# Attention probabilities divided by their sum on GpSimd in place of VectorE

## The chip, the cores and the metric

One core of one Trainium2 chip. The metric is the device time of one execution in microseconds (us). The engines are named as the profile names them: PE is TensorE, DVE is VectorE, ACT is ScalarE, POOL is GpSimd, SP is the engine that issues most DMAs.

## The reference, cut to what matters

A two-layer encoder of 1024 positions and width 1024 in float32. The first layer mixes by windowed attention with 16 query heads on 4 key heads, the second by a gated recurrence; each is followed by layer norm, a gated feed-forward block and a gated side input. The change lies in the attention of the first layer. For each block of 128 queries, with the keys of the block itself and its two neighbours:

```python
s = jnp.einsum('bqhgd,bkhd->bhgqk', qb, kb) * scale
s = jnp.where(valid, s, -jnp.inf)
m = jnp.maximum(s.max(-1, keepdims=True), sink_f)
pr = jnp.exp(s - m)
den = pr.sum(-1, keepdims=True) + jnp.exp(sink_f - m)
return jnp.einsum('bhgqk,bkhd->bqhgd', (pr / den).astype(vb.dtype), vb)
```

Inputs of the attention are x, the weights of the projections and one sink value per head.

## The kernel before, in words

**Matmuls.** Each float32 operand is split into a high part, a cast by ACT (L73), and a low part, the difference, by DVE or POOL (L74, the helper `split`). A product is three matmuls, high by high, high by low and low by high (L349 to L351, the helper `mm3`).

**A group of attention** is one block b of 128 queries and one j, half of the heads (eight heads, as four t by two r). There are sixteen groups. In `scores`, for each t, PE makes two tiles of scores (L562, up to 128x384, in PSUM), and DVE takes scale, mask and row maximum in one pass and puts the scores in SBUF (L564, tiles `pr`; in the first three groups `pq`). When all eight tiles are there, DVE works out the maximum with the sink (L568) and its negative (L570), ACT makes eight exponentials with their row sums (L578), DVE adds the sink's term (L579) and takes the reciprocal (L580, `den`, 128x8), and then eight instructions scale the eight tiles in place, each by one column of `den` (L584). They go through the tiles with t outside and r inside. Blocks 0 and 7 have two key blocks and tiles of 128x256, the other six have three and 128x384: four narrow groups and twelve wide.

**The values** (`values`) of a group come one group later. For each r and each key block, PE transposes four tiles, one for each t, into one PSUM tile (L607, `tps`). ACT and DVE split it into `ph` and `pl` (L73, L74), and PE multiplies both with the value block (L595, L596, tile `o`). ACT and DVE put the result into `of` (L599, L600); its split into `oh` and `ol` ends in POOL (L615 by way of L74; the trace calls these tiles `qh` and `ql`).

**What runs beside it.** `groups` interleaves the scores of one group with the values of the group before, step by step. `weave` puts in 1.15 steps of `more` for each of those: the remaining projections of queries, keys and values, and later the output projection (`aops`, L626). A projected tile of queries or keys is rotated in `rotate`: a shuffle by DVE (L484), a product by POOL (L485), a product and a sum by DVE (L487, L488), and a split that ends in POOL. Of a weight tile `w_qkv` the first half is split by DVE and the second by POOL; of `w_ao` likewise in the first half of the output projection.

**What sets the order.** Each engine runs its queue in order. The order in the queue is not the order of the source alone: when the program is built, the framework places the instructions of each engine by their dependencies and by its own idea of their times. So instructions of `more` stand between those of a group on every engine.

Of the kernel before, what the change touches and what calls it, by code (L numbers as in the profile page):

```python
# [33 lines left out]
def build(tc, xT, pT, wqkv, watt_o, whg, wvh, whg_o, wfi, wfo, wpg, wpp, sink, lbl, ngd, lnp,  # L34
          rope, amask, hmask, ident, outT):
    nc = tc.nc
    sync, act, dve, pool, pe = nc.sync, nc.scalar, nc.vector, nc.gpsimd, nc.tensor
# [8 lines left out]
    with (  # L46
# [16 lines left out]
        def A(name, dt=F32):  # L63
            return ap_.tile([P, HALF], dt, tag="a", name=name)
# [401 lines left out]
        def attention(X, Y):  # L466
            with (
# [70 lines left out]
                def scores(b, j):  # L538
                    h, c = divmod(b, 4)
                    kbs = [kb for kb in (b - 1, b, b + 1) if 0 <= kb < NB]  # L540
                    n = len(kbs)
                    m0 = kbs[0] - (b - 1)
                    if b in (3, 4):
                        kt, ko = Km[j], (b - 3) * P
                    else:
                        kt, ko = Kt[j][h], (kbs[0] % 4) * P
                    kh, kl = (z[:, ko:ko + n * P] for z in kt)
                    mx = tp.tile([P, 2, 4], F32, tag="mx", bufs=3, name="mx")
                    early = j == 0 and b < 3
                    if early:  # L550
                        pq = [qp.tile([P, 4, HALF], F32, tag="q", bufs=8, name=f"pq{r}") for r in range(2)]
                        ss = [pq[r][:, t] for t in range(4) for r in range(2)]
                    else:
                        ss = [A("pr") for _ in range(8)]
                    for t in range(4):
                        yield
                        sp = [aps.tile([P, 3 * P], F32, tag="s", bufs=2, name=f"s{i}") for i in range(2)]
                        qh, ql = (z[:, t, c * P:(c + 1) * P] for z in Q[j][h])
                        for i, (qq, kk) in enumerate(((qh, kh), (qh, kl), (ql, kh))):
                            for r in range(2):  # L560
                                rs = slice(64 * r, 64 * r + 64)
                                pe.matmul(sp[r][:, :n * P], lhsT=qq[rs], rhs=kk[rs], start=i == 0, stop=i == 2)  # L562
                        for r in range(2):
                            dve.tensor_tensor_reduce(ss[2 * t + r][:, :n * P], sp[r][:, :n * P],  # L564
                                                     am[:, m0 * P:(m0 + n) * P], HD ** -0.5, -1e30,
                                                     ALU.add, ALU.max, mx[:, r, t:t + 1])
                    sk = snk[:, 2 * j:2 * j + 2]
                    dve.tensor_tensor(mx, mx, sk, op=ALU.max)  # L568
                    ng = tp.tile([P, 2, 4], F32, tag="ng", bufs=2, name="ng")
                    dve.tensor_scalar_mul(ng, mx, -1.0)  # L570
                    es = tp.tile([P, 2, 4], F32, tag="es", bufs=2, name="es")
                    dve.tensor_tensor(es, sk, mx, op=ALU.subtract)
                    act.activation(es, es, AF.Exp)
                    den = tp.tile([P, 2, 4], F32, tag="den", bufs=2, name="den")
                    for t in range(4):
                        for r in range(2):
                            pt = ss[2 * t + r][:, :n * P]
                            act.activation(pt, pt, AF.Exp, bias=ng[:, r, t:t + 1], accum_out=den[:, r, t:t + 1])  # L578
                    dve.tensor_tensor(den, den, es, op=ALU.add)  # L579
                    dve.reciprocal(den, den)  # L580
                    for t in range(4):
                        for r in range(2):
                            pt = ss[2 * t + r][:, :n * P]
                            dve.tensor_scalar_mul(pt, pt, den[:, r, t:t + 1])  # L584
                    return b, j, kbs, ss

                def values(b, j, kbs, ss):
# [53 lines left out]
                def groups(gs):  # L641
                    prev = None
                    for g in gs:
                        box = []

                        def first(g=g, box=box):
                            box.append((yield from scores(*g)))

                        if prev is None:
                            yield from first()  # L650
                        else:
                            yield from both(first(), values(*prev))
                            seen.add(prev[:2])
                        prev = box[0]
                    yield from values(*prev)
# [682 lines left out]
```

## Time and profile before

| | |
|---|---|
| median of three runs | 2872.57 us (2869.69 to 2874.74) |
| profiled execution | 2872.11 us |
| its span, first to last instruction | 2870.3 us |
| mean granted clock of PE | 0.981 of full speed |

The time of a run is a little longer than the span, which leaves out what lies before the first and behind the last instruction. All times inside the profile count from the span's start. An engine's busy time holds only instructions that compute; what it waited for is inferred from the semaphores.

### The profile page before, as it was taken

To read this page: it belongs to the slowest core of one execution; us is meant where nothing else is said; L and a number is where in the kernel's file an instruction comes from. 1 tells how busy PE (TensorE), PEld (TensorE's weight loads), DVE (VectorE), ACT (ScalarE), POOL (GpSimd) and SP (SyncE) were. 2 spreads that over 40 slices of the span, in tenths; PEclk is the share of its full clock that TensorE was granted. 3 is DMA by queue.
4 is the path that set the end of the run, shared out by engine and by line. 5 is a ranking of instruction groups with operands and counts; after the bars stand their busy time and mean duration, and the time that the engine had idled before them with its cause. 6 is when DMAs were issued, how large, how long until landed. Compare 5 with 4: busy or idle time off the path is not lost.

```text
span 2870.3 us, 37158 instructions
## 1 busy us (share of the span) xinstructions
PE 2711.7 (94%) x12820; PEld 2184.5 (76%) x12820; DVE 2007.5 (70%) x2903; ACT 1287.1 (45%) x2338; POOL 1407.1 (49%) x982
## 2 busy tenths in 40 slices
PE   8999998999999998999998999989989999999998
PEld 6666676788887787787787877878767888878777
DVE  6778887755554657848888888898885554556685
ACT  4555666333333445534444443444553333344453
POOL 4243234756555747653433433331466565566563
PEclk9999999999999999999999999999999999999999
DMA  4111135544445943211111211112355444478243
GB/s 162 50 44 45 51 113 186 168 162 165 148 157 194 358 159 110 85 59 64 56 63 45 74 55 59 60 52 78 111 172 180 158 156 141 157 272 300 82 156 115
DMA packets 194301, 360.35 MB, mean 126 GB/s; under 512 B 22080, under 2 KB 24896, under 8 KB 194112
## 3 DMA queue, kind: packets, MB, share of 16 engines
q1 hardware_dynamic: 150048, 277.74, 29.0%
q10 hardware_dynamic: 44064, 80.24, 7.7%
q8 instruction: 101, 1.65, 0.2%
q14 instruction: 88, 0.72, 0.1%
HBM read 273.47 MB, written 84.41 MB: 125 GB/s over the span
## 4 chain that ended last, share of the span: by engine, by line
PE 33%; DVE 11%; issue 5%; POOL 4%; DMA 3%; ACT 2%; SPq 0%; ACTq 0%; POOLq 0%; DVEq 0%
PE x L349 3%; PE x L351 3%; PE x L350 3%; PE zps L351 2%; PE zps L350 2%; PE zps L349 2%; PE lv L1078 2%; POOL wo L74 2%; PE op L1158 1%; DVE K L1075 1%; PE zy L349 1%; PE zy L351 1%; PE zy L350 1%; DMA wraw<-w 1%; DVE Q L1048 1%
## 5 line engine op out<-in xcount | busy, mean ns | idle before, releaser
L74 POOL TENSOR_TENSOR w_hz<-r_hz,w_hz 128x512 fp32r<-128x512 f32 x128 | 180.3, 1415 | 333.0 <-ACT w_hz L73 322.5
L74 DVE TENSOR_TENSOR wp<-wraw,wp 128x512 fp32r<-128x512 f32 x204 | 216.0, 1059 | 167.0 <-ACT wp L73 137.9
L74 DVE TENSOR_TENSOR hs<-wraw,hs 128x512 fp32r<-128x512 f32 x154 | 206.3, 1356 | 144.7 <-ACT hs L73 141.5
L74 POOL TENSOR_TENSOR wo<-wraw,wo 128x512 fp32r<-128x512 f32 x154 | 226.2, 1481 | 157.4 <-ACT wo L73 153.5
L73 ACT CAST wp<-wraw 128x512 fp32r<-128x512 f32 x204 | 126.6, 622 | 282.3 <-PE x L351 142.4
L349 PE MATMUL x<-xc,wp 128*128 128x512 f32 x528 | 211.2, 401 | 8.0 <-DVE u L757 8.0
L351 PE MATMUL x<-xc,wp 128*128 128x512 f32 x528 | 211.2, 400 | 3.9 <-DVE wp L74 3.9
L349 PE MATMUL zps<-xh_n,w_hz 128*128 128x512 f32 x512 | 212.7, 415 | 0.0
L350 PE MATMUL x<-xc,wp 128*128 128x512 f32 x528 | 210.4, 399 | 0.5 <-DVE xc L74 0.5
L351 PE MATMUL zps<-xh_n,w_hz 128*128 128x512 f32 x512 | 202.7, 396 | 0.0
L350 PE MATMUL zps<-xl_n,w_hz 128*128 128x512 f32 x512 | 201.7, 394 | 0.0
L73 ACT CAST wo<-wraw 128x512 fp32r<-128x512 f32 x154 | 95.4, 620 | 187.8 <-POOL wo L74 114.2
L186 POOL TENSOR_TENSOR wraw<-s,wraw 128x512 f32<-128x512 f32 x36 | 47.6, 1322 | 217.4 <-DVE wp L74 204.8
L349 PE MATMUL ox<-hs,wo 128*128 128x512 f32 x352 | 138.7, 397 | 12.2 <-ACT hs L73 12.2
L351 PE MATMUL ox<-hs,wo 128*128 128x512 f32 x352 | 139.0, 395 | 1.6 <-POOL wo L74 1.6
L350 PE MATMUL ox<-hs,wo 128*128 128x512 f32 x352 | 139.1, 395 | 0.4 <-DVE hs L74 0.4
L349 PEld LDWEIGHTS x<-xc,wp 128*128 128x128 f32 x528 | 100.4, 190 | 34.7 <-ACT wp L73 5.8
L1078 PEld LDWEIGHTS lv<-Q,ks 128*128 128x128 f32 x768 | 97.9, 191 | 37.4 <-issue 23.1
L1070 ACT COPY ks<-K 128x512 f32<-128x512 f32 x96 | 60.5, 631 | 144.7 <-DVE K L1075 111.7
L1078 PE MATMUL lv<-Q,ks 128*128 128x128 f32 x768 | 105.5, 280 | 20.6 <-DVE tot L1089 10.2
L351 PEld LDWEIGHTS x<-xc,wp 128*128 128x128 f32 x528 | 100.4, 190 | 29.4 <-DVE wp L74 4.8
L73 ACT CAST w_hz<-r_hz 128x512 fp32r<-128x512 f32 x128 | 79.0, 618 | 89.6 <-issue 42.4
(377 smaller groups left out, 8475.4 us busy)
## 6 DMA issues: line engine op xcount, KB each, us to landing
wraw<-in_wfi_dram SPq DMA_DIRECT2D x192, 256.0 KB, 3.6
wraw<-in_wfo_dram SPq DMA_DIRECT2D x154, 256.0 KB, 4.0
wraw<-h SPq DMA_DIRECT2D x154, 256.0 KB, 4.8
r_hz<-in_whg_dram SPq DMA_DIRECT2D x128, 256.0 KB, 2.8
wraw<-w SPq DMA_DIRECT2D x88, 256.0 KB, 5.3
w<-wraw ACTq DMA_DIRECT2D x66, 256.0 KB, 2.1
h<-th ACTq DMA_DIRECT2D x66, 256.0 KB, 2.1
r_pg<-in_wpg_dram SPq DMA_DIRECT2D x32, 512.0 KB, 4.2
```

What stands on the lines that cost most here:

```text
L73: act.copy(hi, src)
L74: (eng or dve).tensor_tensor(lo, src, f32(hi), op=ALU.subtract)
L186: pool.tensor_tensor(a11, tmp, a11, op=ALU.subtract)
L349: pe.matmul(ps, lhsT=w[0], rhs=x[0], start=start, stop=False, skip_group_check=free)
L350: pe.matmul(ps, lhsT=w[0], rhs=x[1], start=False, stop=False, skip_group_check=free)
L351: pe.matmul(ps, lhsT=w[1], rhs=x[0], start=False, stop=stop, skip_group_check=free)
L1048: dve.tensor_tensor(Qq[:, 1 - d], qk[:, 0], Fg[:, d], op=ALU.mult)
L1070: act.copy(view(ks, 0, [[2 * B, g], [B, 2], [1, B]]), kv)
L1075: dve.tensor_tensor(kv, kv, view(cur, off + 1, [[2, g], [row - 1, 2], [0, B]]), op=ALU.mult)
L1078: pe.matmul(lv[:, c], lhsT=ks[:, c * P:(c + 1) * P], rhs=view(Qq, c * P, dims), start=True, stop=True)
L1158: pe.matmul(op[:, cs], lhsT=a, rhs=b, start=i == 0, stop=i == len(ops) - 1)
```

## The change

Line 584 is issued to POOL in place of DVE. The operands, the loop around it and everything else in the source stay as they are.

```diff
                     for t in range(4):
                         for r in range(2):
                             pt = ss[2 * t + r][:, :n * P]
-                            dve.tensor_scalar_mul(pt, pt, den[:, r, t:t + 1])
+                            pool.tensor_scalar_mul(pt, pt, den[:, r, t:t + 1])
                     return b, j, kbs, ss
```

## Rows read from the trace of the kernel before

**Rows 1.** The page: the span, and busy us, share and instructions of PE.

```profile
span 2870.3 us, 37158 instructions
PE 2711.7 (94%) x12820; PEld 2184.5 (76%) x12820; DVE 2007.5 (70%) x2903; ACT 1287.1 (45%) x2338; POOL 1407.1 (49%) x982
```

**Rows 2.** One window: length, busy us of five engines, PE clock, DMA share, GB/s.

```profile
60.00:390.00 330.00, 309.09 (x1545) 222.84 (x1546) 263.00 (x685) 189.77 (x478) 102.74 (x81) 0.97 0.16 53
```

**Rows 3.** The instructions of L584: duration ns min/median/max, first and last start.

```profile
L584 DVE TENSOR_SCALAR pr<-pr,den x104: 342/409/1532, 137.1 to 376.2; 128x384 f32<-128x384 f32 x80, 128x256 f32<-128x256 f32 x24
L584 DVE TENSOR_SCALAR pq<-pq,den x24: 340/405/1433, 76.4 to 121.3; 128x384 f32<-128x384 f32 x16, 128x256 f32<-128x256 f32 x8
```

**Rows 4.** PE's waits, 60 to 400 us: us in total, times, longest.

```profile
PE tps L607 <- DVE pr L584: 6.5, 7, 2.0
PE s L562 <- DVE mx L564: 6.4, 3, 4.4
PE o L596 <- DVE pl L74: 5.0, 4, 2.5
PE tps L607 <- DVE pq L584: 3.4, 4, 1.9
PE aops L350 <- POOL ql L74: 0.8, 1, 0.8
```

**Rows 5.** Timeline of DVE: start, duration, instructions.

```profile
76.35 4.22 DVE L584 TENSOR_SCALAR pq<-pq,den 128x256 f32<-128x256 f32 x8
...
88.25 0.72 DVE L484 STREAM_SHUFFLE sw<-qps 128x512 f32<-128x512 f32 x1
...
178.61 4.76 DVE L584 TENSOR_SCALAR pr<-pr,den 128x384 f32<-128x384 f32 x8
...
231.08 5.91 DVE L584 TENSOR_SCALAR pr<-pr,den 128x384 f32<-128x384 f32 x8
...
301.52 2.71 DVE L584 TENSOR_SCALAR pr<-pr,den 128x384 f32<-128x384 f32 x8
...
374.32 2.19 DVE L584 TENSOR_SCALAR pr<-pr,den 128x256 f32<-128x256 f32 x8
```

**Rows 6.** Timeline of POOL: start, duration, instruction, idle time before it and its end.

```profile
89.12 1.29 POOL L485 TENSOR_TENSOR sw<-sw,rt 128x512 f32<-128x512 f32 x1 [10.01 <-DVE sw L484]
...
162.60 0.40 POOL L510 CAST kmh<-kh 128x256 fp32r<-128x256 f32 x1
...
231.19 1.46 POOL L74 TENSOR_TENSOR ql<-ra,qh 128x512 fp32r<-128x512 f32 x1 [3.19 <-ACT qh L73]
232.81 1.29 POOL L74 TENSOR_TENSOR w_qkv<-r_qkv,w_qkv 128x512 fp32r<-128x512 f32 x1 [0.16 <-ACT w_qkv L73]
```

**Rows 7.** Timeline of PE, transposes and value products.

```profile
80.36 0.65 PE L607 MATMUL tps<-idn,pq 128*128 128x128 f32 x2
...
181.78 0.33 PE L607 MATMUL tps<-idn,pr 128*128 128x128 f32 x1 [1.83 <-DVE pr L584]
...
183.52 0.41 PE L607 MATMUL tps<-idn,pr 128*128 128x128 f32 x1
...
237.64 0.80 PE L596 MATMUL o<-pl,v 128*128 128x512 f32 x1 [2.54 <-DVE pl L74]
...
262.64 0.49 PE L596 MATMUL o<-pl,v 128*128 128x512 f32 x1 [1.69 <-DVE pl L74]
...
304.57 0.38 PE L607 MATMUL tps<-idn,pr 128*128 128x128 f32 x2
```

**Rows 8.** Windows behind four of those waits, columns as in rows 2.

```profile
81.00:84.50 3.50, 3.50 (x12) 1.98 (x10) 2.29 (x8) 0.96 (x2) 0.00 (x0) 0.59 0.05 16
182.00:186.50 4.50, 4.50 (x18) 3.43 (x17) 3.20 (x9) 1.50 (x3) 2.05 (x2) 0.62 0.19 62
239.00:242.00 3.00, 3.00 (x14) 2.69 (x13) 2.41 (x6) 2.29 (x5) 1.89 (x2) 0.69 0.00 0
262.70:266.00 3.30, 3.30 (x18) 2.63 (x19) 3.09 (x6) 1.79 (x3) 1.43 (x2) 1.00 0.19 67
```

## The prediction

> **What bounds the kernel now.** The page comes first [rows 1]: TensorE (PE) is busy 94% of the span. So the kernel is bound by PE as a whole, and an edit on DVE or POOL is worth only what PE loses by waiting for them. Next come the windows of the attention stretch, the only one in which the edited line runs [rows 2]: from 60 to 390 us PE is busy 309.09 of 330 us and its granted clock is 0.97 on average; DVE is busy 263.00 us (80%), POOL 102.74 us (31%). PE's idle time there is 20.9 us. A clock of 0.97 means that 3% of the time was lost at the lower of the two levels, 1.2 against 2.4 GHz: some 10 us. So no edit in this stretch that leaves PE's work alone can win more than about 31 us, 1.1% of the time. That is a ceiling, not a forecast.
>
> Then the list of PE's own waits there [rows 4]: 9.9 us go to transposes (tps, L607) that wait for the scaling of L584 (6.5 for the tiles pr, 3.4 for pq), 6.4 us to scores waiting for the reduction L564, 5.0 us to the value product waiting for DVE's split pl. The timelines show why the scalings are late [rows 5, 6, 7]. In the group at 301.52, during which POOL starts nothing, eight scalings of 128x384 take 2.71 us: one every 0.34 us. In the group at 231.08 POOL runs its subtractions beginning at 231.19 and 232.81, and the same eight take 5.91 us. The reader should see both halves of this: the eight are a block in DVE's in-order queue, so whatever stands behind them (pl above all) is late too. The wait of 2.54 us at 237.64 and that of 1.69 us at 262.64 are such pl's behind a block.
>
> What a wait costs beyond itself is in the clock [rows 8]. In the stretches that follow the waits of 1.8 us and more (81 to 84.5 us, 182 to 186.5, 239 to 242) PE's granted clock is 0.59 to 0.69; a fourth like the second begins at 207 and has 0.60. In the stretch behind the wait of 1.69 us at 262.64 it is 1.00. The time lost is the stretch by (1 - clock): 3.5 x 0.41 = 1.4 us, 4.5 x 0.38 = 1.7, 3.0 x 0.31 = 0.9, and for the fourth 4.0 x 0.40 = 1.6.
>
> **The change part by part.** *Removed from DVE:* 128 instructions in 16 groups of eight [rows 3]; the blocks last from about 2.2 to 5.91 us [rows 5], some 60 us of DVE's 263. This alone gives PE nothing except where PE waited for something queued behind a block. Those are the pl waits, 2.54 + 1.69 us and 0.2 us in a third place, 4.4 us of the 5.0 in the list, and the slow clock behind the first: 0.9 us from 239 to 242 and about 0.3 us just before. Together that is 5.6 us, and I take all of it as won, since the list names DVE's pl as what came last there.
>
> *Added to POOL:* the same 128 instructions, at a price that no row shows, since POOL runs no such operation before. From below: one of its casts of 128x256, which also read one tensor and write one, takes 0.40 us where DVE doesn't disturb it [rows 6]; were that all fixed cost, 384 columns would take 0.40 too, and were it all columns, 0.60. From above: its subtractions of 128x512 take 1.29 us, so 384/512 of that is 0.97 us, for an operation with two inputs. I take 0.55 us for 384 columns and 0.40 for 256, in the cast's span and near its upper end, because the scaling reads one tensor as the cast does. For the first instruction I add 0.15 us, the gap between the end of a shuffle on DVE (88.25 + 0.72) and the POOL instruction at 89.12 that it releases [rows 5, 6]. The k-th scaling of a wide group thus ends 0.15 + 0.55k us after the point at which DVE starts today; the seventh, which the last transposes of the first key block need, at 4.0 us; in a narrow group (256 columns) at 2.95 us.
>
> The Trainium skill (GPSIMD Engine Reference, section 4.1 Engine selection) speaks against such a move: elementwise work belongs on VectorE, GpSimd being about twice as slow with two inputs, though roughly at line rate with one. Twice DVE's undisturbed 0.34 would be an estimated 0.68 us, and by the slope worked out below the sum would shrink from 10 to about 2 us. No row here shows which half of the rule holds for a scaling with one scalar per partition; the casts lean to its second half.
>
> *The transposes.* Nine groups have waiting or tight transposes at the head of their values. For each I take when the transposes with t = 3 start today, counted from the start of the block, against 4.0 us (2.95 if narrow) [rows 5, 7]. At 178.61 they start at 183.52, 4.9 us in: 0.9 us won. In the next one, at 203.75 and of the same pattern, they come 5.8 us in: 1.8 won. At 76.35 (narrow; 80.36, 4.0 in): 1.05 won. At 301.52 (304.57, 3.05 in): 0.95 lost. At 374.32, the last group and narrow, 2.0 in: 0.9 lost, with little left to cover it. The other four (100, 118, 158 and 283 us, from 3.5 to 4.1 in) come to 0.95 lost together. Net: 0.95 us won. The gaps are also smaller, since four transposes share them: below the 1.69 us behind which the clock stayed up. So of the three slow stretches at 81, 182 and 207 I count as won what is not already in these figures: 1.4 + 1.1 + 0.8 = 3.3 us.
>
> The SBUF — State Buffer page of the Trainium skill (section Who interferes with whom) says that a DVE instruction using both ports blocks GpSimd entirely and is blocked by it. The trace agrees with 5.91 against 2.71 us for the same block. By it the stretching would vanish with the move; the sum above needs only the blocks as measured.
>
> *What is queued behind it on POOL.* POOL is in order. Its subtractions ql and w_qkv become ready at the same moment as the scalings (231.19 beside 231.08), as the two starts show. Behind eight scalings they come 4.4 us later. Their readers are scores of a later group, the output projection, or the next weight tile. PE waits 0.8 us for POOL in the whole stretch, once [rows 4], and I cost this at nothing, hidden by the projections' matmuls; uncovered it would be up to 4 us a group.
>
> **The sum**, against the profiled execution's own 2872.11 us (span 2870.3), half a microsecond from the runs' median of 2872.57: 5.6 + 0.95 + 3.3 = 9.85 us won, so 2862.3, rounded to 2862. Each 0.1 us on the price of one scaling moves the seventh by 0.7 us in nine groups, 6 us in all; the gain is used up at about 0.71 us.
>
> **The rivals.**
>
> *A: nothing measurable.* The order within each engine's queue is laid out anew when the program is built, for all engines. PE may then wait elsewhere (as it does for 6.4 us on L564) as long as it did. For it: PE is busy 94% anyway. Against it: eleven waits on the scalings and three on a pl behind them, 14 us in all, hang on these blocks alone. Time: 2867 to 2877.
>
> *B, slower: POOL's scaling is dear.* At 0.97 us the seventh ends 6.95 us in, 2.95 us later than in my sum, in nine groups: 26 us, and nine waits beyond 1.8 us with 1.5 us of slow clock each: 13. Time: 2862 + 39 = 2901. It decides from 0.71 us on; at 0.80 it gives 2862 + 15 = 2877 without any slow clock and 2890 with all of it. For it: POOL's subtractions of 1.29 us. Against it: its casts.
>
> *C: POOL's one queue.* If one or two subtractions of 1.29 us stand ahead of the scalings in the nine groups in which both become ready together, transposes come 12 to 23 us later in total: 2874 to 2885. For it: the coincidence in time. Against it: today the block starts 0.11 us before the first of them [rows 5, 6], so the scalings are ready first.
>
> **How the numbers follow.** Forecast 0.40 (own range 2855 to 2869), A 0.25, B 0.22, C 0.13. A change under 0.2% (5.7 us) can't be told from none here. Faster takes 0.36 of the forecast and 0.04 of A: 0.40. Same takes 0.04 of the forecast, 0.20 of A and 0.05 of C: 0.29. Slower is all of B, 0.08 of C and 0.01 of A: 0.31. The range goes from 2855, the forecast's low end, to 2903, just past B at 0.97 us.
>
> **What would show it.** On POOL, L584 at 0.5 to 0.6 us for 384 columns, eight in a row without a subtraction between them; at 0.75 or more the forecast fails. Among PE's waits, pl near zero, tps on POOL's L584 at 5 to 10 us in shorter pieces, and a mean clock from 60 to 390 us of 0.98 or more. DVE's busy time there should fall by some 60 us. Were tps waits at 25 us or more, B or C would hold, told apart by the mean duration and by what stands between the scalings. Were all this as described and the time unchanged, PE's idle time in the stretch would name the new wait.

## The result and the profile after

| | before | after |
|---|---|---|
| median | 2873.18 us (2869.69 to 2874.74, 4 runs) | 2992.30 us (2989.11 to 2993.78, 4 runs) |
| span of the profiled execution | 2870.3 us | 2991.3 us |
| mean granted clock of PE | 0.981 | 0.957 |

The kernel became slower: 1.042 times the time before, 95% interval 1.0407 to 1.0433, some 119 us. The prediction said 2862, range 2855 to 2903.

The first lines of the page of after, beside [rows 1]:

```profile
span 2991.3 us, 37207 instructions
...
PE 2771.3 (93%) x12820; PEld 2214.6 (74%) x12820; DVE 1961.0 (66%) x2775; ACT 1288.2 (43%) x2338; POOL 1549.3 (52%) x1110
```

POOL has 142 us more of work, DVE 46.5 us less, although the 128 scalings took 59.2 us there: other instructions of DVE take longer now, the sum L488 above all (22.9 us in twenty, 15.9 before). The last scaling starts at 495.8 us (376.2 before), so all of the loss lies in the attention. The instructions of L584, beside [rows 3]:

```profile
L584 POOL TENSOR_SCALAR pr<-pr,den x104: 917/1242/1849, 160.8 to 495.8; 128x384 f32<-128x384 f32 x80, 128x256 f32<-128x256 f32 x24
L584 POOL TENSOR_SCALAR pq<-pq,den x24: 922/1237/1706, 78.7 to 139.7; 128x384 f32<-128x384 f32 x16, 128x256 f32<-128x256 f32 x8
```

The median is 1.24 us, that of the wide tiles, and the shortest, 0.92, that of the narrow ones. DVE's undisturbed 0.34 [rows 5] is 3.7 times shorter. The attention as one window, beside [rows 2], 450 us where it was 330:

```profile
60.00:510.00 450.00, 363.94 (x1528) 251.07 (x1529) 214.77 (x555) 189.42 (x475) 246.40 (x209) 0.80 0.12 38
```

PE is idle for 450 - 363.94 = 86 us (21 before), and its granted clock is 0.80 (0.97): of 364 busy us a fifth, 73 us, is lost to the lower level (9 before). That is 65 us more idle and 64 us more of slow clock; together 129, a little above the 120 by which the stretch grew. PE's waits, 60 to 520 us, beside [rows 4]:

```profile
PE tps L607 <- POOL pr L584: 59.0, 42, 2.1
PE tps L607 <- POOL pq L584: 14.1, 12, 2.0
PE s L562 <- DVE mx L564: 6.7, 3, 4.8
PE o L596 <- DVE pl L74: 6.5, 3, 4.0
```

Fifty-four waits of transposes on a scaling, 73.1 us, stand where eleven with 9.9 us stood; every one of the sixteen groups has two to four. The 63 us more are nearly all of PE's added idle time. The waits for pl have not gone. The same list over all engines:

```profile
ACT ph L73 <- PE tps L607: 149.4, 42, 8.6
DVE pl L74 <- ACT ph L73: 74.7, 31, 7.2
```

Before, these two rows had 50.6 and 5.1 us. One group of after shows how the waits come about, in the timeline (start, duration, instruction, idle time before it and what ended it):

```profile
105.72 0.20 DVE L580 RECIPROCAL den<-den 128x8 f32<-128x8 f32 x1
...
106.09 10.18 POOL L584 TENSOR_SCALAR pq<-pq,den 128x384 f32<-128x384 f32 x8 [6.39 <-ACT qh L73]
...
107.39 0.44 PE L607 MATMUL tps<-idn,pq 128*128 128x128 f32 x2 [1.06 <-POOL pq L584]
...
109.33 0.20 DVE L568 TENSOR_TENSOR mx<-mx,snk 128x8 f32<-128x8 f32 x1
...
110.22 0.44 PE L607 MATMUL tps<-idn,pq 128*128 128x128 f32 x2 [1.84 <-POOL pq L584]
...
112.66 0.69 PE L607 MATMUL tps<-idn,pq 128*128 128x128 f32 x2 [1.22 <-POOL pq L584]
...
115.11 0.69 PE L607 MATMUL tps<-idn,pq 128*128 128x128 f32 x2 [1.33 <-POOL pq L584]
...
115.62 1.07 ACT L73 CAST ph<-tps 128x512 fp32r<-128x512 f32 x2 [8.58 <-PE tps L607]
...
116.24 1.29 DVE L74 TENSOR_TENSOR pl<-tps,ph 128x512 fp32r<-128x512 f32 x2 [6.71 <-ACT ph L73]
...
122.35 0.17 DVE L570 TENSOR_SCALAR ng<-mx 128x8 f32<-128x8 f32 x1
...
124.17 0.61 ACT L578 ACTIVATE pq<-pq,ng 128x384 f32<-128x384 f32 x1
```

Read it from the top. POOL's eight take 10.18 us with nothing between them. PE's queue holds the transposes in pairs, one pair for each t (one transpose for each of two key blocks), with at most a few matmuls between two pairs, so PE stops four times. ACT's cast ph stands at the head of ACT's queue for 8.58 us until the last pair is done, and DVE's pl waits behind it. Here the maximum of the *next* group is ready at 109.33 + 0.20, but its negative (L570) stands behind pl and part of a rotation in DVE's queue and comes at 122.35, and its exponentials follow at 124.17.

So the block of one group holds up the reciprocal, and with it the block, of the next. In most groups, however, this goes another way. There are fifteen passages from a group to the next, and in fourteen of them the negative starts 0.2 to 3.5 us after the maximum; it is the maximum itself that is late, because the scores are. The group whose reciprocal starts at 189.64 is of this kind:

```profile
199.16 0.69 PE L607 MATMUL tps<-idn,pr 128*128 128x128 f32 x2 [0.90 <-POOL pr L584]
...
204.34 0.64 PE L562 MATMUL s<-kh,qh 64*128 64x384 f32 x2
...
208.50 0.44 PE L562 MATMUL s<-kh,qh 64*128 64x384 f32 x1
...
210.52 0.15 DVE L568 TENSOR_TENSOR mx<-mx,snk 128x8 f32<-128x8 f32 x1
...
211.19 0.15 DVE L570 TENSOR_SCALAR ng<-mx 128x8 f32<-128x8 f32 x1
```

Three of the four steps of the next group's scores stand behind the waiting transposes in PE's queue, and the maximum comes behind the last of them. In thirteen of the fifteen passages the last scores start after the last waiting transposes. What PE loses there is not made up: the reciprocals are 27.3 us apart on average, where they were 19.9.

Windows around the first of these two groups, beside [rows 8]:

```profile
100.00:106.00 6.00, 6.00 (x31) 3.98 (x30) 4.66 (x18) 5.97 (x20) 0.00 (x0) 1.00 0.16 45
107.00:112.00 5.00, 2.21 (x9) 0.99 (x9) 2.08 (x7) 0.03 (x1) 5.00 (x5) 0.86 0.34 107
112.00:120.50 8.50, 6.51 (x20) 4.95 (x21) 2.71 (x5) 1.07 (x2) 6.81 (x6) 0.50 0.00 0
```

PE was busy throughout at clock 1.00, then 2.21 of 5 us, and then it ran at the lower of its two levels until 120.5.

### The profile page after: what moved, and what is told of

The parts are those of the page before. It is cut to its first block, busy times and chain, and to the rows that moved or that the text cites. A ratio compares the mean times of both kernels' runs of the same rounds, so it can differ in the third digit from the quotient of the medians.

```text
span 2991.3 us, 37207 instructions
## 1 busy us (share of the span) xinstructions
PE 2771.3 (93%) x12820; PEld 2214.6 (74%) x12820; DVE 1961.0 (66%) x2775; ACT 1288.2 (43%) x2338; POOL 1549.3 (52%) x1110
## 4 chain that ended last, share of the span: by engine, by line
PE 34%; DVE 11%; issue 5%; POOL 4%; ACT 2%; DMA 1%; ACTq 0%; POOLq 0%; SPq 0%; DVEq 0%
PE x L349 3%; PE x L351 3%; PE x L350 3%; PE zps L351 2%; PE zps L349 2%; PE zps L350 2%; PE lv L1078 2%; POOL wo L74 2%; PE op L1158 1%; DVE K L1075 1%; PE zy L349 1%; PE zy L351 1%; PE zy L350 1%; DVE Q L1048 1%; PE pgps L350 1%
## 5 line engine op out<-in xcount | busy, mean ns | idle before, releaser
L584 POOL TENSOR_SCALAR pr<-pr,den 128x384 f32<-128x384 f32 (+1 forms) x104 | 122.2, 1194 | 66.5 <-DVE den L580 29.5
```

Of the source, the lines that this page charges most:

```text
L584: pool.tensor_scalar_mul(pt, pt, den[:, r, t:t + 1])
```

## The experiments

The questions were: is it POOL's price, and whose; does the loss lie in the direct waits, in the clock, in what is queued behind the block on POOL, or in the chain from group to group; and does anything win. In the diffs a comment names the kernel that an edit starts from (before or after) and the run that it makes. Letters for theories hold within their group of runs.

**The price.** Three forms of the scaling on POOL. The first leaves out the division by the sum, the third does so for all columns but the first 112.

```diff
-pool.tensor_scalar_mul(pt, pt, den[:, r, t:t + 1])     # after
+pool.tensor_scalar_mul(pt, pt, 0.5)                    # e1_pool_imm
+pool.tensor_tensor(pt, pt, den[:, r, t:t + 1].to_broadcast([P, n * P]), op=ALU.mult)   # e2_pool_bcast
+pool.tensor_scalar_mul(pt[:, :112], pt[:, :112], den[:, r, t:t + 1])   # e3_pool_112
```

> The changed kernel with the scaling on POOL by the constant 0.5 in place of a column of den; the division by the sum is left out. In the changed kernel one scaling takes 1242 ns for 384 columns and 917 to 923 for 256, so 0.27 us plus 2.54 ns per column. If the scalar read from memory makes it dear, the constant brings the row down to the casts' price, 0.5 to 0.6 us, and the time to 2860 to 2890. If the operation itself has this price on POOL, the row stays at 1.2 us; the time stays high too, above 2950, although the scalings no longer wait for the reciprocal.

> The same division on POOL, written as a product of two tensors, den repeated along the columns. Theory of the price: the time follows the row of L584. POOL's two-input rows (1.29 us for 512 columns) give 0.97 us for 384, and if the loss of 119 us grows linearly from the prediction's break-even of 0.71 to 1.24 us, 0.97 us gives 58 us, so about 2930. Rival, the hop between engines with its newly laid out queues: the price doesn't matter, and the time stays within 15 us of 2992.

> The changed kernel with POOL scaling only the first 112 columns of each tile, so the division is left out for the other columns; by 0.27 us + 2.54 ns per column one scaling takes 0.55 us, the price that the prediction had taken. Theory of the price: the prediction's sum holds, 2855 to 2870. Rival, hop and queues: handovers, order and number of instructions are as in the changed kernel, so the time stays above 2940.

Measured: e1_pool_imm 2924.16 us (one run); e2_pool_bcast 2926.78, ratio 1.0195 (1.0166 to 1.0225); e3_pool_112 2937.38, ratio 1.0221 (1.0194 to 1.0249). The rows of L584 in the first, the second and the third:

```profile
L584 POOL TENSOR_SCALAR pr<-pr x104: 845/1169/1567, 139.0 to 426.2; 128x384 f32<-128x384 f32 x80, 128x256 f32<-128x256 f32 x24
```

```profile
L584 POOL TENSOR_TENSOR pr<-pr,den x104: 607/826/1280, 149.9 to 431.6; 128x384 f32<-128x384 f32 x80, 128x256 f32<-128x256 f32 x24
```

```profile
L584 POOL TENSOR_SCALAR pr<-pr,den x104: 554/562/1082, 158.6 to 437.7; 128x112 f32<-128x112 f32 x104
```

The constant costs 1.17 us against 1.24, so it is the operation that is dear and not its scalar from memory. (The time of e1_pool_imm is lower than that suggests, and lower than the 2950 expected; that its scalings wait for no reciprocal is a likely reason, not a shown one.) The same product, as an operation with two inputs, costs 0.83: the dearer-looking form is the cheaper one, and it returns 65 of the 119 us. From 0.917 us (256 columns) and 1.242 (384) come 2.54 ns a column and 0.27 us fixed; the 0.554 us at 112 columns fits that (0.27 + 0.28).

What e3_pool_112 showed besides weighs more. It scales at the price that the prediction took for wide tiles, and its time is 2937 and not 2862. Its block takes 4.33 us where nothing disturbs it; on DVE a block takes 3.7 us on average (59.2 us in sixteen), and single ones 4.76 and 5.91 [rows 5]. Yet it cost some 64 us. Its transposes wait 30.2 us for POOL, in 43 waits, and much of the rest is the clock. In its first group PE stops four times for only 0.49 to 0.74 us. Windows of e3_pool_112, the stops and what follows:

```profile
76.00:81.50 5.50, 2.98 (x13) 1.77 (x12) 1.28 (x6) 2.11 (x6) 4.32 (x9) 0.95 0.00 0
81.50:101.30 19.80, 19.80 (x51) 12.85 (x49) 10.36 (x25) 3.96 (x7) 4.45 (x5) 0.50 0.08 28
```

PE was busy for 2.98 of 5.5 us in four short gaps, and then ran at the lower level for 19.8 us on end, though it was busy all of that time.

**The bounds: no scaling at all, a short one, a long one on DVE.**

```diff
-for t in range(4):                                     # before; e4_none leaves the loop out
-    for r in range(2):
-        pt = ss[2 * t + r][:, :n * P]
-        dve.tensor_scalar_mul(pt, pt, den[:, r, t:t + 1])
-pool.tensor_scalar_mul(pt, pt, den[:, r, t:t + 1])     # after
+pool.tensor_scalar_mul(pt[:, :16], pt[:, :16], den[:, r, t:t + 1])   # e15_pool_16
 dve.tensor_scalar_mul(pt, pt, den[:, r, t:t + 1])      # before
+dve.tensor_scalar_mul(pt, pt, 1.0)                     # e11_dve_twice
```

> The kernel before with the 128 scalings left out, so the division by the sum is left out: what they cost in all where DVE makes them. By the prediction's account, PE's waits behind the blocks (14.3 us) and the slow clock behind four of them (about 6 us) go away: 2850 to 2855. If PE's order soaks up what is freed (rival A of the prediction), no lower than 2866.

> The changed kernel with POOL scaling only 16 columns of each tile (division left out for the others): 0.27 us + 16 x 2.54 ns = 0.31 us, less than DVE's 0.34. Rival, the hop between engines and the queues laid out for POOL cost by themselves: 2915 or more, like the 112 columns. Theory that lateness costs and nothing else: the block is over in 2.6 us, so between the kernel without scalings (2846) and the one before (2871).

> The kernel before with every scaling on DVE followed by a second one by 1.0: the price doubled, 0.68 us for each tile undisturbed, without any change of engine. Theory that lateness of the scalings costs PE, wherever they are made: as dear as the run with 112 columns on POOL, whose tiles cost 0.56 us, so 2920 to 2950. Rival, the hop from DVE to POOL and back to PE costs by itself: the DVE version pays only its longer blocks, 2875 to 2890.

Measured: e4_none 2846.29, ratio 0.9906 (0.9891 to 0.9921); e15_pool_16 2888.30, ratio 1.0068 (1.0048 to 1.0088); e11_dve_twice 2905.01, ratio 1.0118 (1.0098 to 1.0138). So nothing that one does to the scalings could win more than some 25 to 27 us. Eight POOL instructions of 0.33 us (16 columns), a block no longer than DVE's undisturbed one, cost 16 to 20 us more than DVE's. That is the nearest measure of what PE's new order and the longer hop cost by themselves (from the start of the reciprocal to the first scaling 0.37 us, 105.72 to 106.09). And a block made twice as long on DVE costs 33 us, so the length of the block matters there too. But length isn't all: that block takes 4.9 us undisturbed and costs half of what 4.33 us on POOL cost (64). The times of e15_pool_16 and e11_dve_twice lie between the ranges of both theories.

**Where the loss lies: PE's order.** Three rearrangements of after, and one control.

```diff
-for t in range(4):                                     # after
-    for r in range(2):
+for r in range(2):                                     # e9_pool_r_outer
+    for t in range(4):
+for _ in range(3):                                     # e6_lag: ahead of the loop in values
+    yield
-weave(groups(gs), more(), 1.15)
+weave(groups(gs), more(), 0.8)                         # e6_lag too; e12_before_lag: both edits on before
```

> The changed kernel with the loop over r outside and t inside: POOL makes first the four tiles that the first transposes read, so these wait for four scalings, 5 us, and not for seven, 8.7 us. Theory: 3.7 us less in each of sixteen groups, and shorter slow stretches: 2930 to 2955. Rival, the price is paid in POOL's queue and not at the first transposes: within 10 us of 2992.

> The changed kernel with the values of a group begun three steps later, and 0.8 in place of 1.15 steps of other work for each step, so that the same work is spread over the longer way. Theory: PE loses because its queue has the transposes right behind the reciprocal, while POOL needs 10 us for a block; with three more steps ahead of them, some 4 us of matmuls, the waits on L584 fall from 73 us to 30 or less and the clock recovers, 2900 to 2940. Rival, POOL's scalings as a bound of the whole chain of groups: whatever stands where, the time stays at 2980 or above.

> The same two edits on the kernel before, scalings on DVE: the control for the later start. If it wins by covering the 14 us of waits behind the blocks, 2850 to 2860; if the longer way to the last group costs as much as it covers, 2870 to 2885.

Measured: e9_pool_r_outer 2985.88, ratio 1.0396 (1.038 to 1.0411); e6_lag 2959.55, ratio 1.0297 (1.0277 to 1.0318); e12_before_lag 2879.46, ratio 1.0029 (1.0019 to 1.0039). PE's waits in e9_pool_r_outer:

```profile
PE tps L607 <- POOL pr L584: 28.3, 37, 3.0
PE s L562 <- DVE mx L564: 22.7, 5, 6.0
PE o L596 <- DVE pl L74: 11.2, 3, 7.5
PE tps L607 <- POOL pq L584: 7.7, 11, 1.3
```

With the four scalings of r=0 first, the direct waits are half of what they were (36 of 73 us), and the time falls by 6 us alone: of the 37 us that PE no longer waits at the transposes, 21 come back at the scores and at pl, and the granted clock from 60 to 510 us is 0.81. So shortening the direct waits doesn't by itself return them. Beginning the values three steps later, with fewer steps of `more` between, wins 33 us from after, where it costs 8 in the kernel before: a longer block wants more cover. The waits at the transposes fall to 25.6 us, as expected, but the waits for pl rise to 30.6, and 2960 is far from the 2900 to 2940 expected.

**The clock.** Added transposes (the same ones again, with no other effect than to keep PE busy in the gaps), in after and in e3_pool_112.

```diff
-pe.transpose(tps[:, t * P:(t + 1) * P], ss[2 * t + r][:, i * P:(i + 1) * P], idn)
+for _ in range(K if r == 0 and i == 0 else 1):   # K = 9: e13_fill; K = 5: e14_fill_112
+    pe.transpose(tps[:, t * P:(t + 1) * P], ss[2 * t + r][:, i * P:(i + 1) * P], idn)
```

> The changed kernel with each transpose of the first key block of r = 0 made nine times over into the same place, so that PE has work while it waits for the next scalings: 512 further transposes of 128 columns. Theory of the clock: of the 119 us about half is slow clock behind clusters of short waits (granted 0.80 on average from 60 to 510 us); with the waits filled the clock goes above 0.9 and the time falls to 2930 to 2965, though PE has some 60 us more work. Rival, only the waits count: the added work is hidden at best, 2985 to 3020.

> The same with the kernel that scales 112 columns on POOL (division left out for the others), each such transpose made five times: 256 further transposes, 30 us of work at full clock. That kernel took 2937, with granted 0.87 from 60 to 450 us and 19.8 us on end at 0.50 with PE busy throughout. Theory of the clock: below 2925, with the clock above 0.92. Rival, waits and work alone: 2937 to 2965.

Measured: e13_fill 3001.67, ratio 1.0452 (1.0433 to 1.0471), against 1.042 of after; e14_fill_112 2917.5, ratio 1.016 (1.014 to 1.0181), against 1.0221 of e3_pool_112. The window of e13_fill, and then that of e14_fill_112 (60 to 450, where e3_pool_112 has clock 0.87):

```profile
60.00:510.00 450.00, 374.46 (x2006) 273.18 (x2007) 206.96 (x548) 187.40 (x471) 241.45 (x207) 0.92 0.11 37
```

```profile
60.00:450.00 390.00, 355.03 (x1848) 257.87 (x1849) 220.79 (x571) 196.87 (x488) 173.82 (x213) 0.95 0.14 47
```

At 112 columns more work made the kernel 18 to 20 us faster, and from 60 to 450 us PE lost 18 us to the lower level, where it lost 44. So the lower clock cost at least that much of its 64 us, unless the added instructions also changed the order in the queues for the better, which no run excludes. At full length the clock came back to 0.92 (30 us lost, where it was 73), and the time rose by 9 us. Part of the added work stands on the path itself (behind the last of the four waits), and by PE's account some 60 us of added work took the place of 43 us of slow clock and some 10 us of idle time. So this doesn't show that the slow clock was free, nor what it cost; it shows that filling the gaps in this way wins nothing at full length.

**POOL's own queue.** What stands behind the block on POOL is above all rotate's product sw, for which DVE's sum L488 waits 22.1 us in 11 waits in after, and DVE's reductions queue up behind that. So it was taken off POOL, in after and in before.

```diff
-pool.tensor_tensor(sw, sw, rt[h][1], op=ALU.mult)
+dve.tensor_tensor(sw, sw, rt[h][1], op=ALU.mult)   # e16_sw_dve on after, e17_before_sw_dve on before
-split(hi, lo, a, pool)
+split(hi, lo, a)                                   # e18_rot_dve: both lines, on after
```

> The changed kernel, with the product of rotate (L485, sw times the table) made by DVE in place of POOL, so that it no longer stands behind POOL's block of scalings. Theory Q (what is queued behind the block carries much of the loss: sw late, so DVE's sum L488 late, so the reductions L564 late, so the next group late): DVE's waits for sw on POOL (22.1 us in 11) vanish and the time falls by 25 us or more, to 2965 or less. Theory T (the loss lies in the transposes that wait for POOL's scalings and in the clock behind them): the scalings keep 1.24 us, the waits of the transposes stay at about 70 us, and only some of the 6.7 us of scores waiting for reductions is won, while DVE has more to do: 2980 to 3000.

> Control: the kernel before (scalings on DVE) with the same edit of L485. Its DVE waits for sw on POOL 9.5 us in 8, and gets 20-odd products of about 0.6 to 1.3 us more. Theory Q: the edit is worth little here, within 8 us of before (2865 to 2881), so that a gain in the changed kernel belongs to the block on POOL. Theory T: the same for this one; it only serves to take the edit's own worth out.

> The changed kernel with the product of rotate and the subtraction of rotate's split (L489) both made by DVE, so that of the projections only the second half of each w_qkv stays behind POOL's block. Theory Q: below the run with L485 alone by another 5 to 15 us, since ql is no longer late. Theory T: no faster than the changed kernel by more than 10 us, or slower, since DVE has more to do and POOL's eight scalings still take about 10 us.

Measured: e16_sw_dve 2978.57, ratio 1.0374 (1.0359 to 1.039); e17_before_sw_dve 2861.42, ratio 0.9963 (0.9949 to 0.9977); e18_rot_dve 2976.79, ratio 1.0362 (1.0344 to 1.0379). PE's waits in e16_sw_dve:

```profile
PE tps L607 <- POOL pr L584: 58.8, 42, 2.5
PE tps L607 <- POOL pq L584: 14.4, 11, 2.5
PE o L595 <- ACT ph L73: 2.1, 3, 1.4
PE s L562 <- DVE mx L564: 1.6, 2, 1.4
```

The edit wins 14 us in after and 10.5 in before: some 3 us belong to the block. Theory Q falls (and T's range is missed by 1.4 us), though the waits that it named were real and went away. The transposes wait as long as before (73.2 us). With ql off POOL too, e18_rot_dve is 2 us faster still, which the spread of its runs (2968 to 2980) covers; it lies outside what both theories expected.

**Half the change, and three that win.**

```diff
-dve.tensor_scalar_mul(pt, pt, den[:, r, t:t + 1])      # before
+(pool if r else dve).tensor_scalar_mul(pt, pt, den[:, r, t:t + 1])   # e5_pool_r1
+if r: act.activation(pt, pt, AF.Copy, scale=den[:, r, t:t + 1])      # e7_dve_act
+else: dve.tensor_scalar_mul(pt, pt, den[:, r, t:t + 1])              # e20_act_sw_dve: with L485 on DVE
```

> Half of the change: the scalings with r=1 go to POOL, those with r=0 stay on DVE. POOL's price of one should stay at about 1.24 us. Theory T (the transposes that wait for POOL's scalings, one after another, make the loss): the transposes of r=0 wait for DVE's four, which are done in 2 to 3 us, and those of r=1 come later in PE's queue than POOL's four take (5 us), so most of the 73 us of waits and of the slow clock is gone: 2865 to 2895. Theory P (any work of 1.24 us an instruction on POOL costs its length): half of the 119 us, 2925 to 2940.

> A version meant to shorten the block without POOL: the scalings with r=0 stay on DVE, those with r=1 go to ACT (a copy with the scale taken from den). If the block on DVE is what costs, as the run without scalings bounds it (27 us at most), half of it off DVE gives 2860 to 2870. If ACT's copies make its own high parts (L73) and exponentials late, it ends at 2875 to 2900.

> The two edits that each made the kernel before faster, together: scalings with r=1 on ACT, and the product of rotate (L485) on DVE. If what they win is different waits, the gains of 8.4 and 10.5 us add up: 2850 to 2856. If both win the same (the few us of waits behind a block on DVE, and the slow clock behind them), about 2860.

One more run made no difference: the exponentials, sums, reciprocals and scalings of r=0 ahead of all those of r=1, on DVE.

```diff
+for r in range(2):                                     # e10_halves, on before
+    for t in range(4):
+        pt = ss[2 * t + r][:, :n * P]
+        act.activation(pt, pt, AF.Exp, bias=ng[:, r, t:t + 1], accum_out=den[:, r, t:t + 1])
+    dve.tensor_tensor(den[:, r], den[:, r], es[:, r], op=ALU.add)
+    dve.reciprocal(den[:, r], den[:, r])
+    for t in range(4):
+        pt = ss[2 * t + r][:, :n * P]
+        dve.tensor_scalar_mul(pt, pt, den[:, r, t:t + 1])
```

> The kernel before with everything behind the maxima done for r = 0 first and then for r = 1: four exponentials, sum, reciprocal, four scalings on DVE. The tiles of the first transposes are then ready some 3 us (four exponentials) and three scalings (1 to 2 us) earlier. Theory that the lateness of the scalings is what costs: most of the 25 us that leaving them out wins, 2850 to 2862. Rival: sixteen more small instructions on DVE and a wait there for ACT twice in each group, 2870 to 2885.

Measured: e5_pool_r1 2888.54, ratio 1.0065 (1.0046 to 1.0084); e7_dve_act 2863.56, ratio 0.9973 (0.9961 to 0.9984); e20_act_sw_dve 2858.85, ratio 0.9959 (0.9944 to 0.9973); e10_halves 2871.55, ratio 1.0002 (0.9991 to 1.0014). The rows of L584 in e5_pool_r1, and its largest wait of PE:

```profile
L584 POOL TENSOR_SCALAR pr<-pr,den x52: 918/1244/1762, 135.8 to 390.4; 128x384 f32<-128x384 f32 x40, 128x256 f32<-128x256 f32 x12
L584 DVE TENSOR_SCALAR pr<-pr,den x52: 336/723/1098, 135.9 to 388.7; 128x384 f32<-128x384 f32 x40, 128x256 f32<-128x256 f32 x12
```

```profile
PE o L596 <- DVE pl L74: 19.3, 14, 3.4
```

POOL's price is the same, 1.24 us, and half as many cost 18 us, not half of 119 (Theory P falls). The transposes that come first wait for DVE's four, POOL's four are done by the time r=1 is read, and no wait of a transpose on POOL is among PE's larger ones. DVE's scalings take 0.72 us beside POOL's, where they took 0.41, and pl behind them is late. The gains of e7_dve_act (8.4 us) and e17_before_sw_dve (10.5) don't add up: both together win 12. All three gains are small, 0.3 to 0.4%; each interval ends below 1.

## Why the prediction was wrong

**Two steps failed: the price of one scaling on POOL, and the account of the transposes that wait for it.** First the price. The prediction took 0.55 us for 384 columns, between the cast's 0.40 and 0.97 from a two-input subtraction [rows 6]; it measured 1.24, above its upper bound. The bound was built on the idea that an operation with one input costs no more than one with two. On POOL the two-input product does lie inside the bounds (0.83) and the one-input scaling doesn't. The cast was the wrong relative: it is another operation. The Trainium skill (GPSIMD Engine Reference, section 4.1 Engine selection) says that elementwise work belongs on VectorE, which this case bears out, and puts GpSimd at about half speed with two inputs and roughly at line rate with one. The second half doesn't hold here: 1.24 us against DVE's 0.34 for one input.

**The price alone doesn't give 2992.** In the prediction's own sum, with its hop of 0.15, it moves the seventh scaling to 0.15 + 7 x 1.24 = 8.83 us, 4.83 later than taken, in nine groups: 43 us, and 13 for the clock: 2862 + 56 = 2918. The other 74 us lie in the account of the transposes, and that account fails at the price taken, too: e3_pool_112, at 0.56 us a scaling, took 2937, 75 us above the forecast. In PE's own account of after, idle time grew by 65 us where this sum has 43, and slow clock by 64 where it has 13. Three parts of the account failed; how the 74 divide among them was not measured.

- *"Nine groups."* All sixteen groups wait, 54 times. The prediction held the transposes where the kernel before had them in PE's queue. There four groups (137, 231, 257 and 315 us) have 16 to 22 other matmuls between the reciprocal and the first transposes, and none of them waits. In after at most four matmuls stand between two transposes that wait.
- *Smaller gaps keep the clock up.* It expected four shared gaps to stay "below the 1.69 us behind which the clock stayed up", and in rival B allotted 1.5 us of slow clock to a wait. The four gaps of 0.49 to 0.74 us in e3_pool_112 were followed by 19.8 us at 0.50. The slow clock of after is 73 us, 64 more than before and five times the 13 allotted.
- *What is late next.* The prediction asked what is queued behind the scalings on POOL, and not what is queued behind the transposes. On PE these are the next group's scores, as the timeline from 199 to 211 us shows; in the group from 105 to 125 us it is the next group's negative maximum on DVE, behind pl. So one group's lateness is the next one's start. That the pl waits would go (5.6 us) failed as well: PE waits 6.5 us for pl, and pl waits 74.7 us for ph. The timelines show this chain; no run cut it alone.

**What held.** The ceiling of 31 us: without scalings the kernel wins 25 to 27. What is queued behind the block on POOL was costed at nothing, and e16_sw_dve with its control puts the part of sw in it at some 3 us. Rival C's subtractions ahead of the scalings hardly occur: in fourteen of sixteen groups the block starts 0.36 to 0.38 us behind the start of the reciprocal, in the other two at 0.66 and 0.76. Rival B had the mechanism and the sign; its price stopped at 0.97 us and its count at nine groups. The stretching of DVE beside POOL, for which the prediction named the SBUF — State Buffer page of the Trainium skill (section Who interferes with whom), came back where both work at once: 0.72 us against 0.41 in e5_pool_r1. In after it may also be why DVE was freed of 46.5 us and not of the 60 foreseen.

**What stays open.** How the 119 us divide between idle time and clock: the sums (65 and 64 us) say where PE's time went, not what each would return if it were cured alone. At 112 columns the clock was worth at least 18 us; at full length it could not be told apart. Nor was the cost of the move itself isolated, that of the longer hop and of the queues laid out anew: e15_pool_16 puts it at 16 to 20 us, and the 31 us between e3_pool_112 and e11_dve_twice, with blocks of like length on POOL and on DVE, suggest more.

## What to carry to other kernels

Before an operation is moved to an engine that has never run it, time that very operation there: neither the number of its inputs nor a cast of the same size bounds it. When a block of work on the path between two stages grows, list what stands behind its *readers* in every in-order queue, and see whether the next round's start is among it; if so, the growth is paid once a round and not only at the first wait. If work must leave a busy engine, try the part that is read last: half of these scalings, those with r=1, cost 18 us on POOL and not 119, and won 8 on ACT.

## What the runs showed of the hardware

- POOL's one-input scaling: 0.27 us and 2.54 ns a column (1.24 us for 128x384), with a constant 1.17; the same product with two inputs, one of them broadcast, 0.83.
- PE's granted clock can stay at the lower level for 19.8 us in which PE is busy without a gap (81.5 to 101.3 us of e3_pool_112), after four gaps of which none was longer than 0.74 us.
- Keeping PE busy with useless transposes brought the clock from 0.87 to 0.95 and the time down by 18 to 20 us at 112 columns, and from 0.80 to 0.92 without any gain at full length.
